# Shift product, state tables and transposes ahead of a scan, in another order on TensorE and VectorE

## The chip, the core and the metric

One core of a Trainium2 chip runs the kernel. The metric is the device time of one execution in microseconds (us), as the median of several runs; a profiled execution of the same program gives the trace. TensorE is PE in the profile (its weight loads are PEld), VectorE is DVE, ScalarE is ACT, GpSimd is POOL, and SyncE is SP, which issues nearly all DMA transfers.

## The reference

One layer of a hybrid decoder, for 1024 positions of width 1024. The part that matters here is the start of the mixer:

```python
mod = (c_act @ w_mod[l] + b_mod[l])[:, None, :]
sh1, sc1, g1, sh2, sc2, g2 = jnp.split(mod, N_MOD, axis=-1)
h = _rms(x, norm1_w[l]) * (1 + sc1) + sh1
proj = h @ w_in[l]
u, q, k, v = jnp.split(proj, [...], axis=-1)
y_ssm = _s5(u, ...)          # 32 groups of 16 channels, 64 complex states each
q, k = rms per head; y_attn = _swa_sink(q, k, v, rel_bias, sinks[l])   # window 128, 8 heads
# in _s5, per group: s[t] = A s[t-1] + B u[t] (complex, diagonal A), y = Re(C s) + D u, then GELU, GLU
x = x + g1 * (concat(rms(y_ssm), rms(y_attn)) @ w_out[l])
# then a gated MLP (width 2816) with a causal convolution of width 3
```

## The kernel before

Everything is float32; a product is made of three products of rounded halves ("hi" and "lo", `mm3`), so each weight or activation tile is split: ACT casts the hi part, DVE subtracts to get the lo part (`split`). Eight PSUM banks are handed out round robin: `mbank` from banks 0 to 3, `abank` from banks 4 to 6.

The stage up to the scan works as follows (lines of the kernel before).

- The loop over the eight 128-row blocks of x (from L239) forms scaled x, the columns sc1 of the modulation, the sums of squares (banks 6, 7), and the first six of eight projections of u. The positions are taken with stride 8: projection j holds positions j, j+8, and so on.
- The normalisation factor `rstd` is made by ACT and DVE in two halves (`rsqrt_mean`, L187). Four DVE transposes (L273) turn it into a column per position, `rc`. Only with `rc` can a projection bank be drained into U (`u_out`, L277). Projections j=6 and j=7 use bank 6 and bank 0 again (L285), so j=7 needs bank 0 drained.
- The columns sh1 of the modulation are eight more DVE reductions over rows of `w_mod`, loaded into three buffers in turn (`emit_mod`, L178, called at L294). They become `shs`, hi and lo (L297, L298). The shift product (`shift_u`, L300) multiplies them with the u weights; DVE reduces it to `Bu`, the bias of u.
- The state tables: A's powers (`PWr`, `PWi`) and B in discrete form (`Bb`, `Bsw`), then four large outer products on DVE (`outer`, called at L437), "table 0" to "table 3", in buffers A5 to A8 (`IB`); each is two products and a sum, with the next buffer as temporary. On PE their transposes W (`emit_wj`, eight of them, drained by ACT into A9 to A12) and the transposes of U (`emit_ut`, eight, drained by ACT with the bias `Bu`, L543) feed the injection products (from L571), whose drain is the scan's input `SC` in buffer S16.
- The C tables (`CAt`, from L589) are five buffers of outer products on DVE, in A5 to A8 and A4, so after the W transposes have read tables 0 to 3. From them PE makes the kernels of the chunk (`ka`), which a transfer takes to DRAM (`kd`, L641).
- The heads: k, v and four pairs of query heads, six of them (`head`), each 2 x 24 products of 512 columns, with weights in U0 to U3, DVE and ACT work on each result (`head_out`), and the queries in `qn` (W1, U4, U5 and others). The scan is 18 calls of `cmac` (from L704), seven DVE instructions each, with temporaries `mt` in buffer A12.

Buffers are named by a tag; a new tile under the tag of an older one waits for the older one's last reader or writer. What is written to the queue of an engine runs in order. That order is chosen ahead of time by a planner that simulates the program with its own costs, in which earlier lines have precedence where nothing else is said. `tc.issue_after(i)` puts instructions of the engine of `i` behind `i` in that engine's queue and binds no other engine. `pe.pin(True)` makes PE keep the written order among the instructions so marked (they show as L99, others as L97). From the shift product to the end of the injection PE is pinned; there `next(h0)` puts one step of a head between: first a head's small row products (`head_w`), then three products per step.

Of the kernel before, what the change touches and what calls it, by code (L numbers as in the profile page):

```python
# [14 lines left out]
ADD, SUB, MUL, MAX, MIN = ALU.add, ALU.subtract, ALU.mult, ALU.max, ALU.min  # L15

L = 1024
D = 1024
# [44 lines left out]
def hymba_kernel(ctx, tc, xT, c, wmod, wu, wkvq, small, consts, relb, pq, wglu, wout, wup, wdn, out):  # L63
# [4 lines left out]
    bank = [pp.tile([128, 512], F32, name=f"bk{i}") for i in range(8)]  # L68
    SIZES = {"HA": 2048, "HB": 2048, "S16": 4096, "XQ": 4096}

    def new(tag, dt=F32):
        return pool.tile([128, SIZES.get(tag, 1024)], dt, tag=tag, name="t" + tag)
# [14 lines left out]
    vec, act, pol, sync = nc.vector, nc.scalar, nc.gpsimd, nc.sync  # L87
# [29 lines left out]
    def tt(eng, o, a, b, op):  # L117
        return eng.tensor_tensor(out=o, in0=a, in1=b, op=op)  # L118
# [7 lines left out]
    def stt(o, a, s, b, op0, op1):  # L126
        return vec.scalar_tensor_tensor(out=o, in0=a, scalar=s, in1=b, op0=op0, op1=op1)  # L127
# [24 lines left out]
    def gh(ap):  # L152
        return ap.rearrange("p (g h) -> p g h", h=16)
# [8 lines left out]
    def S(name, j=0, n=None):  # L162
        o, w = SMALL[name]
        return sm[:, o + j:o + (w if n is None else j + n)]
# [10 lines left out]
    mod = pool.tile([128, 48], F32, name="mod")  # L175
# [11 lines left out]
    def rsqrt_mean(o, t_, ps, n):  # L187

        act.activation(out=o, in_=ps, func=AF.Abs_reciprocal_sqrt, scale=1.0 / n, bias=eps)
        act.activation(out=t_, in_=o, func=AF.Square, scale=math.sqrt(0.5 / n))  # L190
        stt(t_, ps, n * 1e-6, t_, ADD, MUL)
        return stt(o, t_, -1.5, o, ADD, MUL)
# [3 lines left out]
    def abank():  # L196
        ab[0] = (ab[0] + 1) % na[0]
        return bank[4 + ab[0]]
# [9 lines left out]
    def mbank():  # L208
        mb[0] = (mb[0] + 1) % 4
        return bank[mb[0]]  # L210
# [4 lines left out]
    def evac(o, i, key):  # L215
        evc[key] = evc.get(key, -1) + 1
        cpy(pick("E" + key, evc[key]), o, i)
# [21 lines left out]
    for k in range(8):  # L239
# [12 lines left out]
        lasth = stt(lo.r, xk, mods[:, k:k + 1], hi.f, MUL, SUB).ins  # L252
# [12 lines left out]
    rstd = new("X6")  # L265
    rc = new("A4")[:, 0:256].rearrange("p (j x) -> p j x", x=32)
    rtmp = new("A11")
    for h in range(2):
        hs = slice(h * 512, h * 512 + 512)
        normed1 = rsqrt_mean(rstd[:, hs], rtmp[:, hs], bank[6 + h], D).ins  # L270
    for q in range(4):
        qs = slice(32 * q, 32 * q + 32)
        vec.transpose(out=rc[qs], in_=rstd[qs, 256 * q:256 * q + 256].rearrange("p (i j) -> p j i", j=8))  # L273
    U = new("S16")[:, 0:4096]
    Uv = U.rearrange("p (g d h) -> p g d h", d=8, h=16)

# [17 lines left out]
            emit_mod(k, mst[k % 3], cact)  # L294
    shs = pool.tile([128, 16], F32R, name="shs")
    shr = RT(shs.rearrange("p (k s) -> p k s", s=2))
    act.copy(shr.r[:, :, 0], mod[:, 0:8])  # L297
    tt(vec, shr.r[:, :, 1], mod[:, 0:8], shr.f[:, :, 0], SUB)  # L298

    def shift_u():  # L300
        b = mbank()
        for k in range(8):
            s_ = [shs[:, 2 * k + i:2 * k + i + 1].to_broadcast([128, 128]) for i in range(2)]
            pe.matmul(b, s_[0], wus[k][0].r, start=(k == 0), stop=False)
            pe.matmul(b, s_[0], wus[k][1].r, start=False, stop=False)
            pe.matmul(b, s_[1], wus[k][0].r, start=False, stop=(k == 7))
        tmp = new("A9")[:, 0:512]
        tt(vec, gh(tmp), gh(b), S("mod16").rearrange("p (o h) -> p o h", o=1).to_broadcast([128, 32, 16]), MUL)
        vec.tensor_reduce(out=Bu, in_=gh(tmp), axis=mybir.AxisListType.X, op=ADD)

# [105 lines left out]
    def outer(eng, o, tmp, g0, ng, nd, u, v):  # L416
        o = o.rearrange("p (g d h) -> p g d h", d=nd, h=16)
        tmp = tmp.rearrange("p (g d h) -> p g d h", d=nd, h=16)
        shp = [128, ng, nd, 16]

        def bx(w_):
            return gh(w_)[:, g0:g0 + ng, :].rearrange("p g (o h) -> p g o h", o=1).to_broadcast(shp)

        def by(w_):
            return w_[:, g0:g0 + ng, 0:nd].rearrange("p g (d o) -> p g d o", o=1).to_broadcast(shp)

        tt(eng, o, bx(u), by(PWr), MUL)
        tt(eng, tmp, bx(v), by(PWi), MUL)
        return tt(eng, o, o, tmp, ADD).ins

    IB = [new(f"A{5 + i}") for i in range(4)]
    hp = ctx.enter_context(ExitStack())
    hp.enter_context(tc.high_priority(0))
    for i in range(4):
        tmp = new("A10") if i == 3 else IB[i + 1]
        with tc.issue_after(normed1 if i > 1 else lasth):
            built = outer(vec, IB[i], tmp, 8 * i, 8, 8, Bb, Bsw)  # L437
    hp.close()

# [65 lines left out]
    def head(t):  # L505
        w = head_w(t)
        yield
        for h in range(2):
            b = mbank()
            for k in range(8):  # L510
                head_mm(b, w, k, halves[h])
                if k == 7:
                    with pe.pin(False):
                        head_out(t, h, b)
                yield


    pst = ExitStack()
    pst.enter_context(pe.pin(True))
    shift_u()  # L520
    h0 = itertools.chain(*[head(t) for t in range(4)])
    next(h0)

    WJt = [new(f"A{9 + i}") for i in range(4)]

    def emit_wj(i):
        b = abank()
        for q in range(4):
            g = 4 * i + q
            pe.transpose(b[:, q * 128:(q + 1) * 128], IB[g // 8][:, (g % 8) * 128:(g % 8 + 1) * 128], ident)  # L530
        evac(WJt[i // 2][:, (i % 2) * 512:(i % 2 + 1) * 512], b, "W")
    UTt = [None] * 4

    def emit_ut(i):
        if i % 2 == 0:
            UTt[i // 2] = new(f"A{i // 2}")
        b = abank()
        for q in range(4):
            g = 4 * i + q
            pe.transpose(b[:, q * 128:(q + 1) * 128], U[:, g * 128:(g + 1) * 128], ident)  # L540
        for q in range(4):
            g = 4 * i + q
            act.activation(  # L543
                out=UTt[i // 2][:, (g % 8) * 128:(g % 8 + 1) * 128].rearrange("p (r q) -> p q r", r=8), in_=b[:, q * 128:(q + 1) * 128].rearrange("p (q r) -> p q r", r=8),
                func=AF.Identity, bias=Bu[:, g:g + 1],
            )

    for i in range(8):
        emit_ut(i)
        if i == 3:  # L550
            next(h0)
    for i in range(8):
        emit_wj(i)

    def UT(g):
        return UTt[g // 8][:, (g % 8) * 128:(g % 8 + 1) * 128]
# [66 lines left out]
    sync.dma_start(out=vdv[:, :, 128:256], in_=mid.rearrange("p (h v) -> p h v", h=8))  # L623


    ka = new("A12")
    kav = ka.rearrange("p (i d h) -> p i d h", d=8, h=16)
    for i2 in range(2):
        b = abank()
# [10 lines left out]
    for q in range(4):  # L640
        sync.dma_start(out=kd[:, 8 * q:8 * q + 8, 112:240],  # L641
                       in_=ka[32 * q:32 * q + 16, :].rearrange("p (g x) -> p g x", x=128))
# [72 lines left out]
    for h in range(2):  # L715
        for i in range(4):
            q_ = newr(f"H{8 + 4 * h + i}")
            for kv in range(2):
                p0, p1 = slice(kv * 64, kv * 64 + 64), slice(64 - kv * 64, 128 - kv * 64)
                q = q_[:, kv * 512:kv * 512 + 512]  # L720
# [73 lines left out]
    for h in range(2):  # L794
        hs = slice(h * 512, h * 512 + 512)
# [44 lines left out]
    for n in range(8):  # L840
        av = bank[2]
        for kv in range(2):
# [6 lines left out]
            for i2 in range(2):  # L849
# [6 lines left out]
                for i1 in range(2):  # L856
                    i = 2 * i2 + i1
                    vec.tensor_tensor_reduce(  # L858
                        out=P[:, i, :], in0=b[:, i1 * 256:i1 * 256 + w_], in1=Tb[kv][:, i, 256 - w_:256],
# [398 lines left out]
    for s_, (c_, i, p) in enumerate(steps):  # L1258
# [27 lines left out]
        if p == ps_[1] and pend:  # L1286
            put(*pend)
            h, dd = DEST[pend[0]]
# [114 lines left out]
```

## Time and profile before

| | before |
|---|---|
| median of 3 runs | 1131.26 us (1129.86 to 1134.01) |
| profiled execution | 1135.45 us, span 1133.7 us |
| busy, share of the span | PE 92%, DVE 81%, ACT 51%, POOL 24% |
| mean granted TensorE clock | 0.964 |

The profile's times count from the first instruction of the span. The line of a row is that of the instruction in the kernel, which may be a helper: L118 is any two-operand DVE instruction, L127 a scalar-tensor-tensor one, L133 a copy by ACT. In tile names the buffer's number is left out, so tA may be A0 or A12, and tS is S16, the scan's buffer after the injection and U before it.

### The profile page before, as it was taken

The numbers are of one execution on the slowest core, as the hardware profiler recorded it, in microseconds if no ns is written. First come the engines' busy times: TensorE is split into PE (matmuls) and PEld (weight loads), VectorE is DVE, ScalarE is ACT, GpSimd is POOL, SyncE is SP. The second block draws the span as 40 slices with busy tenths as digits, with TensorE's granted clock in tenths as the row PEclk, the third lists the DMA queues.
The fourth block names the chain that finished last, engine by engine and source line by source line (L and its number), as shares of the span: only waits on it lengthen the run. The fifth ranks groups of instructions, "written<-read, shape, count | busy, mean of one in ns | idle before, by whom it ended". The sixth has DMA issues, their size and how long they took to land.

```text
span 1133.7 us, 13323 instructions
## 1 busy us (share of the span) xinstructions
PE 1042.0 (92%) x4676; PEld 820.0 (72%) x4676; DVE 916.1 (81%) x1516; ACT 579.4 (51%) x1013; POOL 274.9 (24%) x166
## 2 busy tenths in 40 slices
PE   6979999477979999959999999999999999989998
PEld 4867777275646677647888888888888778768876
DVE  7984599947879787788778887978796887997985
ACT  5325343457788357735454544554554574434342
POOL 0000000001233202681221222222222033654541
PEclk9989999678999999969999999999999999999999
DMA  9421517004017966322223223242221439622012
GB/s 358 157 93 38 111 56 91 3 29 158 19 38 180 289 185 164 112 93 75 93 75 123 100 95 128 88 154 71 93 84 69 167 141 413 152 39 37 1 38 111
DMA packets 49637, 128.13 MB, mean 113 GB/s; under 512 B 6273, under 2 KB 14241, under 8 KB 49570
## 3 DMA queue, kind: packets, MB, share of 16 engines
q1 hardware_dynamic: 44962, 118.89, 31.4%
q0 software_dynamic: 4608, 8.39, 4.6%
q8 instruction: 36, 0.59, 0.2%
q14 instruction: 31, 0.25, 0.1%
HBM read 105.28 MB, written 21.99 MB: 112 GB/s over the span
## 4 chain that ended last, share of the span: by engine, by line
PE 63%; DVE 26%; DMA 4%; ACT 3%; issue 2%; POOL 1%; SPq 0%; DVEq 0%; ACTq 0%; POOLq 0%
PE bk L97 59%; DVE tA L118 6%; PE bk L99 4%; DVE tH L118 4%; DVE tU L118 3%; DVE tX L127 3%; DMA tW<-in_dram 3%; DVE tS L118 2%; DVE tX L118 1%; DMA tX<-in_dram 1%; DVE tX L180 1%; ACT tU L133 1%; DVE tH L858 1%; ACT tA L543 1%; DVE tXQ L127 1%
## 5 line engine op out<-in xcount | busy, mean ns | idle before, releaser
L97 PE MATMUL bk<-tA,tU 128*128 128x512 f32 x516 | 126.3, 393 | 0.0
L97 PE MATMUL bk<-tU,tU 128*128 128x512 f32 x516 | 121.9, 390 | 1.5 <-DVE tU L118 1.3
L97 PE MATMUL bk<-tH,tU 128*128 128x512 f32 x477 | 117.8, 394 | 0.0
L97 PEld LDWEIGHTS bk<-tU,tU 128*128 128x128 f32 x516 | 96.5, 188 | 23.4 <-DVE tU L118 2.6
L97 PEld LDWEIGHTS bk<-tA,tU 128*128 128x128 f32 x516 | 96.8, 188 | 22.2
L97 PEld LDWEIGHTS bk<-tH,tU 128*128 128x128 f32 x477 | 88.9, 188 | 19.8 <-issue 1.0
L127 DVE SCALAR_TENSOR_TENSOR tX<-tH,sm,tX 128x1023 f32<-128x1023 f32 x66 | 98.2, 1488 | 4.6 <-ACT tX L1129 4.5
L97 PE MATMUL bk<-tA,tXQ 128*128 128x512 f32 x300 | 74.0, 393 | 1.9 <-ACT tH L1082 1.9
L133 ACT CAST tU<-tW 128x512 fp32r<-128x512 f32 (+1 forms) x67 | 47.2, 711 | 53.7 <-DMA tW<-in_dram 21.8
L99 PE MATMUL bk<-tH,tU 128*128 128x512 f32 x267 | 65.5, 400 | 3.5 <-DVE tU L118 2.4
L97 PEld LDWEIGHTS bk<-tA,tXQ 128*128 128x128 f32 x300 | 56.2, 188 | 15.1 <-ACT tH L1082 2.3
L97 PE MATMUL bk<-tXQ,tH 128*128 128x256 f32 (+2 forms) x224 | 52.3, 377 | 15.6 <-DVE att L858 8.9
L118 POOL TENSOR_TENSOR tU<-tW,tU 128x512 fp32r<-128x512 f32 x25 | 36.5, 1469 | 117.2 <-ACT tU L133 110.1
L97 PEld LDWEIGHTS bk<-tXQ,tH 128*128 128x128 f32 x224 | 45.0, 269 | 26.0 <-DVE att L858 13.4
L118 POOL TENSOR_TENSOR tH<-tH,att 128x1024 f32<-128x1024 f32 (+1 forms) x9 | 18.1, 2016 | 188.3 <-DVE att L870 168.8
L99 PEld LDWEIGHTS bk<-tH,tU 128*128 128x128 f32 x267 | 50.1, 191 | 17.1 <-DVE tU L118 3.7
L118 POOL TENSOR_TENSOR tXQ<-tW,tXQ 128x512 fp32r<-128x512 f32 x12 | 49.2, 4107 | 52.2 <-ACT tXQ L133 37.0
L118 DVE TENSOR_TENSOR tX<-tX,tX 128x512 f32<-128x512 f32 (+1 forms) x61 | 58.4, 959 | 1.2 <-DMA tX<-in_dram 0.3
L97 PE MATMUL bk<-tH,tA 128*128 128x512 f32 (+1 forms) x156 | 55.5, 488 | 2.3 <-DVE tH L118 1.1
L118 DVE TENSOR_TENSOR tU<-tW,tU 128x512 fp32r<-128x512 f32 (+2 forms) x43 | 37.9, 882 | 20.9 <-ACT tU L133 20.2
L118 POOL TENSOR_TENSOR tU<-tX,tU 128x512 fp32r<-128x512 f32 x19 | 31.2, 1644 | 81.6 <-ACT tU L133 67.5
L118 DVE TENSOR_TENSOR tU<-tX,tU 128x512 fp32r<-128x512 f32 x37 | 29.6, 807 | 23.9 <-ACT tU L133 23.9
(354 smaller groups left out, 2417.1 us busy)
## 6 DMA issues: line engine op xcount, KB each, us to landing
tW<-in_dram SPq DMA_DIRECT2D x49, 512.0 KB, 3.4
tX<-in_dram SPq DMA_DIRECT2D x47, 512.0 KB, 3.4
tS<-in_dram SPq DMA_DIRECT2D x30, 512.0 KB, 6.3
gd<-tX SPq DMA_DIRECT2D x22, 512.0 KB, 2.9
tA<-in_dram SPq DMA_DIRECT2D x12, 512.0 KB, 10.0
tH<-in_dram SPq DMA_DIRECT2D x12, 512.0 KB, 4.3
tH<-gd SPq DMA_DIRECT2D x8, 512.0 KB, 9.5
tA<-gd SPq DMA_DIRECT2D x8, 512.0 KB, 10.5
```

The lines of the kernel that those rows point to most:

```text
L97: return f(*a, **k)
L99: i = f(*a, **k)
L118: return eng.tensor_tensor(out=o, in0=a, in1=b, op=op)
L127: return vec.scalar_tensor_tensor(out=o, in0=a, scalar=s, in1=b, op0=op0, op1=op1)
L133: act.copy(o, i)
L180: vec.tensor_tensor_reduce(out=st, in0=st, in1=ca, scale=1.0, scalar=S("b_mod", j, 1), op0=MUL, op1=ADD, accum_out=mod[:, j:j + 1],)
L543: act.activation(out=UTt[i // 2][:, (g % 8) * 128:(g % 8 + 1) * 128].rearrange("p (r q) -> p q r", r=8), in_=b[:, q * 128:(q + 1) * 128].r ...
L858: vec.tensor_tensor_reduce(out=P[:, i, :], in0=b[:, i1 * 256:i1 * 256 + w_], in1=Tb[kv][:, i, 256 - w_:256], scale=1.0, scalar=S("sink", 4 ...
```

## The change

Four edits:

1. The point `normed1` moves from the end of the normalisation to the last of the four transposes, so that the eight reductions for sh1 stand behind the transposes in DVE's queue. Table 2 need no longer stand behind `normed1`, only behind the last activation block; table 3's temporary is A12 in place of A10.
2. `shs` is made in two halves of four columns; the shift product's temporary is A3 in place of A9.
3. On PE, W transposes 0 to 5 come first, then the shift product, then U transposes 0 to 3, W transposes 6 and 7, two head steps, U transposes 4 to 7. Before it was: shift product, one head step, U transposes 0 to 3, one head step, U transposes 4 to 7, W transposes 0 to 7.
4. The kernels of the chunk, `ka`, lie in buffer U4 in place of A12. U4 holds B's table before that and a query of head 3 after it.

```diff
     for h in range(2):
         hs = slice(h * 512, h * 512 + 512)
-        normed1 = rsqrt_mean(rstd[:, hs], rtmp[:, hs], bank[6 + h], D).ins
+        rsqrt_mean(rstd[:, hs], rtmp[:, hs], bank[6 + h], D)
     for q in range(4):
         qs = slice(32 * q, 32 * q + 32)
-        vec.transpose(out=rc[qs], in_=rstd[qs, 256 * q:256 * q + 256].rearrange("p (i j) -> p j i", j=8))
+        normed1 = vec.transpose(out=rc[qs], in_=rstd[qs, 256 * q:256 * q + 256].rearrange("p (i j) -> p j i", j=8)).ins
...
-    act.copy(shr.r[:, :, 0], mod[:, 0:8])
-    tt(vec, shr.r[:, :, 1], mod[:, 0:8], shr.f[:, :, 0], SUB)
+    for k in range(0, 8, 4):
+        act.copy(shr.r[:, k:k + 4, 0], mod[:, k:k + 4])
+        tt(vec, shr.r[:, k:k + 4, 1], mod[:, k:k + 4], shr.f[:, k:k + 4, 0], SUB)
...
-        tmp = new("A9")[:, 0:512]
+        tmp = new("A3")[:, 0:512]
...
     for i in range(4):
-        tmp = new("A10") if i == 3 else IB[i + 1]
-        with tc.issue_after(normed1 if i > 1 else lasth):
+        tmp = new("A12") if i == 3 else IB[i + 1]
+        with tc.issue_after(normed1 if i > 2 else lasth):
             built = outer(vec, IB[i], tmp, 8 * i, 8, 8, Bb, Bsw)
...
-    shift_u()
     h0 = itertools.chain(*[head(t) for t in range(4)])
-    next(h0)
...
+    for i in range(6):
+        emit_wj(i)
+    shift_u()
     for i in range(8):
         emit_ut(i)
         if i == 3:
+            emit_wj(6)
+            emit_wj(7)
             next(h0)
-    for i in range(8):
-        emit_wj(i)
+            next(h0)
...
-    ka = new("A12")
+    ka = new("U4")
```

## The prediction

> **What bounds the kernel now.** I read the page's head, then a table of busy times by stretch (columns: length, busy time of PE, PEld, DVE, ACT, POOL, granted clock, share and rate of the DMA engines), cut where the character of the work changes. The fence below it has two rows of the same table for the instructions on the scan's buffer alone (columns in the same order).
>
> ```profile
> span 1133.7 us, 13323 instructions
> core 0: us, PE busy (x) PEld busy (x) DVE busy (x) ACT busy (x) POOL busy (x), PEclk, DMA share, GB/s
> 85.00:106.00 21.00, 19.46 (x107) 15.48 (x107) 6.32 (x23) 10.95 (x35) 0.15 (x1) 0.92 0.15 50
> 106.00:122.00 16.00, 15.81 (x170) 12.84 (x170) 15.26 (x17) 8.75 (x25) 0.32 (x2) 1.00 0.52 80
> 122.00:138.00 16.00, 16.00 (x142) 12.78 (x141) 3.13 (x6) 5.43 (x8) 0.00 (x0) 1.00 0.40 101
> 138.00:198.00 60.00, 58.62 (x297) 45.22 (x295) 59.26 (x141) 25.49 (x38) 0.00 (x0) 1.00 0.45 73
> 198.00:232.00 34.00, 13.40 (x32) 7.54 (x32) 33.37 (x80) 13.17 (x21) 0.00 (x0) 0.59 0.04 4
> ```
>
> ```profile
> 138.00:198.00 60.00, 0.00 (x0) 0.00 (x0) 33.82 (x92) 0.00 (x0) 0.00 (x0) 1.00 0.45 73
> 198.00:232.00 34.00, 0.00 (x0) 0.00 (x0) 13.67 (x36) 0.52 (x1) 0.00 (x0) 0.59 0.04 4
> ```
>
> The reader is to see three things. From 138 to 232 VectorE (DVE) is full: 59.26 + 33.37 = 92.6 of 94 us, of which 47.5 are the scan. Ahead of that, from 85 to 138, DVE works 6.32 + 15.26 + 3.13 = 24.7 of 53 us: it waits 28 us for a chain on TensorE (PE) and ScalarE (ACT). So the full stretch starts late, and what brings its start forward moves its end, if the work in it keeps up. The next view is the timeline, engine by engine (start, length, instructions, in brackets the idle time before and who ended it). First the chain to the scan on PE:
>
> ```profile
> 62.42 0.90 PE L97 MATMUL bk<-tU,tHA 128*128 128x512 f32 x3
> 65.35 3.09 PE L97 MATMUL bk<-tXQ,tH 128*128 128x512 f32 x12
> 73.84 1.67 PE L97 MATMUL bk<-tU,tHA 128*128 128x512 f32 x3 [5.40 <-ACT tS L279]
> 78.71 3.09 PE L97 MATMUL bk<-tXQ,tH 128*128 128x512 f32 x12
> 83.34 0.73 PE L99 MATMUL bk<-tU,shs 128*128 128x512 f32 x2 [1.54 <-ACT shs L297]
> 85.53 3.89 PE L99 MATMUL bk<-tU,shs 128*128 128x512 f32 x10 [1.46 <-DVE shs L118]
> 89.25 2.94 PE L99 MATMUL bk<-tXQ,shs 128*128 128x512 f32 x12
> 96.04 3.14 PE L97 MATMUL bk<-tH,tU 128*128 128x512 f32 x13
> 104.13 0.66 PE L99 MATMUL bk<-cn,tA 128*128 128x128 f32 x4 [0.45 <-ACT tA L543]
> 109.15 2.35 PE L99 MATMUL bk<-tA,tA 128*64 128x128 f32 x32
> 118.70 2.02 PE L99 MATMUL bk<-tA,tA 128*64 128x128 f32 x32
> 193.63 3.42 PE L97 MATMUL bk<-tH,tU 128*128 128x512 f32 x14
> ```
>
> In order: projection j=6 (62.42 to 68.44), j=7 (73.84 to 81.80), the shift product (83.34 to 92.19), U and W transposes (93 to 109.15), four groups of injection products (109.15 to 120.72), then heads until about 197. DVE and ACT beside them:
>
> ```profile
> 60.09 0.69 DVE L127 SCALAR_TENSOR_TENSOR tA<-bk,tA 128x512 f32<-128x512 f32 x1 [4.12 <-ACT tA L190]
> 63.79 0.68 DVE L127 SCALAR_TENSOR_TENSOR tX<-tA,tX 128x512 f32<-128x512 f32 x1
> 66.81 1.28 DVE L180 CUSTOM_DVE_ANT_0 tA<-tA,tX,sm 128x1024 f32<-128x1024 f32 x1
> 68.02 1.22 DVE L118 TENSOR_TENSOR tA<-Bbt,PWr 128x1024 f32<-128x1024 f32 x1
> 69.15 2.35 DVE L118 TENSOR_TENSOR tA<-tU,PWi 128x1024 f32<-128x1024 f32 x2
> 71.74 1.27 DVE L273 STREAM_TRANSPOSE tA<-tX 32x256 f32<-32x256 f32 x2
> 77.94 1.41 DVE L122 TENSOR_SCALAR tS<-bk,tA 128x512 f32<-128x512 f32 x2
> 105.85 1.21 DVE L118 TENSOR_TENSOR tA<-tU,PWr 128x1008 f32<-128x1008 f32 x1 [10.82 <-PE bk L99]
> 124.33 0.69 DVE L118 TENSOR_TENSOR tX<-bk,tX 128x512 f32<-128x512 f32 x1 [2.53 <-PE bk L99]
> 129.09 0.29 DVE L118 TENSOR_TENSOR tA<-tA,ddt 128x128 f32<-128x128 f32 x1 [4.07 <-ACT tA L133]
> 130.88 0.69 DVE L127 SCALAR_TENSOR_TENSOR tX<-bk,tX 128x512 f32<-128x512 f32 x1 [1.50 <-ACT tX L190]
> 138.00 1.43 DVE L118 TENSOR_TENSOR tA<-tS,ep 128x256 f32<-128x256 f32 x4 [4.91 <-DMA kd<-tA]
> 164.89 0.68 DVE L118 TENSOR_TENSOR tU<-bk,tX 128x512 f32<-128x512 f32 x1
> ```
>
> ```profile
> 73.10 3.00 ACT L279 ACTIVATE tS<-bk,tA 128x512 f32<-128x512 f32 x5 [11.80 <-DVE tA L273]
> 83.09 0.20 ACT L297 CAST shs<-mod 128x8 fp32r<-128x8 f32 x1 [0.56 <-DVE mod L180]
> 93.74 2.58 ACT L543 ACTIVATE tA<-bk,Bu 128x128 f32<-128x128 f32 x8 [0.39 <-DVE Bu L309]
> 99.65 6.49 ACT L543 ACTIVATE tA<-bk,Bu 128x128 f32<-128x128 f32 x24 [3.33 <-PE bk L99]
> 105.85 4.13 ACT L133 COPY tA<-bk 128x512 f32<-128x512 f32 x8
> 120.71 1.19 ACT L133 COPY tS<-bk 128x448 f32<-128x448 f32 x4 [2.34 <-PE bk L99]
> ```
>
> The last row's scan input is complete at 121.90; yet the scan's first instruction starts at 138.00, released by the transfer of the kernels of the chunk out of A12, the buffer that the scan's temporaries take next.
>
> **The change, part by part, with its sum.**
>
> *Transposes ahead of the modulation columns, table 2 ahead of both.* Now DVE does the second normalisation step until 64.47, three column reductions (1.21 us apart), table 2 (68.02 to 71.50, 3.48 us), and only then the last two transposes, until 73.01. ACT's drain of bank 0 waits 11.80 us for them and PE 5.40 us for the drain. After the change table 2 may go into DVE's 4.12 us of idle time before 60.09, where its 3.48 fit, and the reductions stand behind the transposes, which end at 64.47 + 1.27 = 65.7. The first drain takes 3.00 / 5 = 0.6, so bank 0 is free at 66.3, before j=6 ends at 68.44: j=7 follows with no gap. It takes 7.96 us now, j=6 took 6.02; without a gap I take 6.02, so j=7 ends at 74.46 in place of 81.80. Gain 7.3, cover 2.1 us (66.3 to 68.44). If the idle time can't take table 2, it goes behind the transposes, and the gain still stands.
>
> *W transposes 0 to 5 ahead of the shift product, which comes in halves.* Eight took 104.13 to 109.15, 5.0 us; six cost 3.8, and PE reaches the shift at 78.2. Is its input there? From 65.7 DVE has two drains (1.41), eight reductions (9.7) and table 3 (3.5): 80.3 at the latest, the first four columns before 76. So the first half product (12 instructions, 2.94) runs until 81.2 and the second finds its columns. The halves add one ACT copy (0.20) and one small subtraction, nothing on this path. The reloads that SyncE (SP) issues for reductions 3 to 7 still follow the reductions that free their three buffers; they move with these, and no other transfer of SP or GpSimd (POOL) is passed. The shift ends at 78.2 + 2 x 2.94 = 84.1 in place of 92.19.
>
> *From the shift to the scan's input.* Bu comes 1.55 us after the shift's end now (92.19 to 93.74), so ACT starts on the U transposes at 85.6. It is the bound there: 32 x 0.27 (6.49 / 24) + two W drains at 0.52 = 9.7, so 95.3. In the trace a group of 24 later head products (one row of it at 96.04) is ahead of some U transposes and ACT idles 3.33 for it; I expect half, since the same PE gap is shorter. Injection starts near 97 in place of 109.15, and with the same 12.75 us to the last drain (109.15 to 121.90) the scan's input is complete at 109.8: gain 12.1. The C tables (DVE, 15.26 us in 106 to 122) no longer wait for all W transposes (the 10.82 us row): the first two can run once the early W transposes have read their buffers, the rest behind W 6 and 7; all are done before 109.
>
> *Kernels of the chunk in U4.* The scan no longer waits for their transfer (4.91). The waits of 2.53, 4.07 and 1.50 before it were also time in which nothing else was ready, because A12 was taken; together 13.0 us in which the scan can now run. The buffer's next user is head 3's query, first written at 164.89, about 27 us behind that transfer; were the cover gone, DVE would stop there for what is missing.
>
> *Sum at the end of the full stretch.* DVE's work behind the scan's input is 3.13 + 92.6 = 95.8; from 109.8 without idle it ends at 205.6, against 232: 26 us. PE sets another limit: its heads end near 197 now, 88 us behind the injection's start; 97 + 88 = 185. Behind them DVE still has what is in 198 to 232 without the scan, 33.37 - 13.67 = 19.7, and some 3 us of latency: 208, so 24 us. I take the later one, 208, and off its 24 us another 2 for the order that the planner will not find: 22. Everything behind 232 starts from this work and PE is the bound of most of it, so I carry all of it to the end. The profiled execution took 1135.45 us, 1.75 around its span of 1133.7; it becomes 1113.5. It lies 4.2 above the median, 1131.26; measured from the median the forecast is 1109. Bounds of what the trace can't show: 7 us (the j=7 gap alone) to 31 (y products start as soon as the scan's 47.5 us are through, ahead of the last heads' outputs).
>
> [...] U and W transposes cycle three PSUM banks, each waiting for an ACT drain of 1.1 us; the granted clock in the like stretch, 106 to 122, was 1.00. [...]
>
> **The rivals.**
> 1. *Scan queued behind head 0.* DVE takes its queue in order. If the planner leaves head 0's output chain ahead of the scan, the waits of 2.53, 4.07 and 1.50 return, 8.1 us: gain 14, 1117. For it: that is the order now. Against: now the scan was not ready before.
> 2. *Everything early.* Gain 31, 1100; for it, the 47.5 us of scan fit well before 185; against, the heads come first in program order.
> 3. *Scan starves the heads.* While the scan fills DVE from 109.8, PE still needs DVE for weight splits and drains of the heads. If the scan stands in the queue as one block of 47.5 us, and two free banks hold 12 us of head products (24 each, at 2.94 / 12), PE stops 35 us: heads end at 220, the stretch at 243, 11 us later than now: 1142. It cancels the gain from a stop of 24 us on, and a stop of 18 to 30 us reads as no change. Against it: in 138 to 198 the two kinds of work stand mixed, 33.82 of 59.26, and PE is busy 58.62 of 60.
> [...]
>
> **How the numbers follow.** A difference under 0.5% (5.7 us) can't be told from none. Forecast (gain 16 to 28): 0.59. Rival 1: 0.14. Rival 2: 0.10. Rival 4: 0.04. Rival 3 as no change: 0.07, as slower: 0.06. Faster is 0.59 + 0.14 + 0.10 + 0.04 = 0.87. The range 1100 to 1123 takes in the forecast, rivals 1 and 4 and half of rival 2: 0.82.
>
> **What would show it.** Right: j=7 starts within 0.5 us of j=6's end and takes about 6 us; the shift product follows W transposes with no wait for its columns and ends near 84; injection starts at 95 to 99; the scan's first instruction starts near 110, released by ACT's drain and not by a transfer; DVE is over 95% busy from there to about 208, and the heads' last product ends near 185. Wrong: reductions or C tables ahead of the shift's columns, so that PE waits there; the scan behind a head output that waits for PE; PE idle for several us between 110 and 185 for a split on DVE; or a later stage that hands the microseconds back.

## The result, and the profile after

The changed kernel takes 1117.19 us (median of 4 runs, 1115.47 to 1119.89), against 1131.69 (median of 4, 1129.86 to 1134.01) for the kernel before beside it: ratio 0.9873, 95% interval 0.9846 to 0.99, a gain of 14.5 us. The profiled execution took 1116.85 us. The table of busy times, cut where the prediction cut it (length, busy PE, PEld, DVE, ACT, POOL, granted clock, DMA share and rate), and below it three stretches of the same kernel for instructions on the scan's buffer alone:

```profile
span 1115.1 us, 13349 instructions
core 0: us, PE busy (x) PEld busy (x) DVE busy (x) ACT busy (x) POOL busy (x), PEclk, DMA share, GB/s
85.00:106.00 21.00, 17.10 (x85) 13.45 (x84) 14.98 (x34) 7.13 (x21) 0.00 (x0) 0.86 0.16 50
106.00:122.00 16.00, 15.06 (x162) 11.88 (x162) 5.91 (x11) 8.19 (x29) 0.48 (x3) 1.00 0.47 76
122.00:138.00 16.00, 16.00 (x142) 12.64 (x141) 15.42 (x37) 7.10 (x13) 0.00 (x0) 1.00 0.40 104
138.00:198.00 60.00, 58.90 (x300) 46.02 (x299) 57.84 (x138) 25.01 (x38) 0.00 (x0) 1.00 0.42 71
198.00:232.00 34.00, 27.82 (x171) 22.52 (x172) 28.24 (x71) 22.99 (x35) 0.00 (x0) 0.80 0.14 25
```

```profile
122.00:138.00 16.00, 0.00 (x0) 0.00 (x0) 11.12 (x28) 0.94 (x4) 0.00 (x0) 1.00 0.40 104
138.00:198.00 60.00, 0.00 (x0) 0.00 (x0) 32.46 (x89) 0.00 (x0) 0.00 (x0) 1.00 0.42 71
198.00:232.00 34.00, 12.70 (x64) 10.33 (x64) 4.89 (x11) 4.18 (x4) 0.00 (x0) 0.80 0.14 25
```

The gain is visible in one row. From 122 to 138 DVE is busy 15.42 us, where it was 3.13 before, and 11.12 of them are scan. PE is as full as before (16.00), so the heads lose nothing by it. From 198 to 232 PE is busy 27.82 us, where it was 13.40: the y products (PE's products with the scan's states, the 64 PE instructions on the scan's buffer) already run there. From 85 to 106, however, PE is busy less than before (17.10, was 19.46). The timeline shows why; PE first (start, length, instructions, in brackets the idle time before and who ended it):

```profile
69.77 1.45 PE L97 MATMUL bk<-tU,tHA 128*128 128x512 f32 x3 [1.72 <-ACT tS L279]
77.33 3.14 PE L99 MATMUL bk<-cn,tA 128*128 128x128 f32 x24
80.23 0.71 PE L99 MATMUL bk<-tU,shs 128*128 128x512 f32 x2
83.74 4.14 PE L99 MATMUL bk<-tU,shs 128*128 128x512 f32 x10 [2.80 <-DVE shs L118]
88.75 0.73 PE L99 MATMUL bk<-tXQ,shs 128*128 128x512 f32 x2 [0.87 <-ACT shs L298]
91.02 4.04 PE L99 MATMUL bk<-tXQ,shs 128*128 128x512 f32 x10 [1.55 <-DVE shs L118]
109.53 0.43 PE L99 MATMUL bk<-tA,tA 128*64 128x128 f32 x2
196.12 0.44 PE L97 MATMUL bk<-tH,tU 128*128 128x512 f32 x1
211.17 0.63 PE L97 MATMUL bk<-tA,tS 128*128 128x128 f32 x2
```

```profile
59.70 0.69 DVE L127 SCALAR_TENSOR_TENSOR tA<-bk,tA 128x512 f32<-128x512 f32 x1 [4.08 <-ACT tA L190]
62.88 1.22 DVE L118 TENSOR_TENSOR tA<-Bbt,PWr 128x1024 f32<-128x1024 f32 x1
67.62 1.31 DVE L273 STREAM_TRANSPOSE tA<-tX 32x256 f32<-32x256 f32 x2
82.41 1.20 DVE L118 TENSOR_TENSOR tA<-tU,PWr 128x1008 f32<-128x1008 f32 x1
83.53 0.15 DVE L118 TENSOR_TENSOR shs<-mod,shs 128x4 fp32r<-128x4 f32 x1
83.60 2.32 DVE L118 TENSOR_TENSOR tA<-tU,PWi 128x1008 f32<-128x1008 f32 x2
89.50 1.22 DVE L118 TENSOR_TENSOR tU<-tW,tU 128x1024 fp32r<-128x1024 f32 x1
90.81 0.15 DVE L118 TENSOR_TENSOR shs<-mod,shs 128x4 fp32r<-128x4 f32 x1
122.31 1.43 DVE L118 TENSOR_TENSOR tA<-tS,ep 128x256 f32<-128x256 f32 x4 [10.30 <-ACT tS L133]
```

```profile
98.06 3.32 ACT L542 ACTIVATE tA<-bk,Bu 128x128 f32<-128x128 f32 x12 [2.84 <-DVE ep L118]
121.74 1.19 ACT L133 COPY tS<-bk 128x448 f32<-128x448 f32 x4 [2.35 <-PE bk L99]
219.36 1.28 ACT L759 ACT_TABLE_LOAD   x1
234.28 1.28 ACT L868 ACT_TABLE_LOAD   x1
503.30 1.28 ACT L1213 ACT_TABLE_LOAD   x1 [1.01 <-DVE tX L127]
```

The shift product does follow the W transposes at 80.23, but stands three times for its columns, and ends at 95.06 (91.02 + 4.04), 2.9 us later than before. On DVE, C tables (the 128x1008 rows) and a weight split stand between the reductions and the subtractions that complete `shs`. The injection starts at 109.53 (before 109.15). The scan nevertheless starts at 122.31, 15.7 us earlier, released by ACT's drain of its own input: nothing stands between the input and the scan any more. The three table loads on ACT mark the first gelu (before at 236.00), the first exponential of the attention (before at 253.60), and the first Silu of the MLP (before at 523.81). The last row of the PE rows above is the first of the y products, at 211.17; in the kernel before it was this one:

```profile
234.59 0.63 PE L97 MATMUL bk<-tA,tS 128*128 128x128 f32 x2
```

### The profile page after: what moved, and what is told of

It reads as the page before. It is cut to its first block, busy times and chain, and to the rows that moved or that the text cites. A ratio compares the mean times of both kernels' runs of the same rounds, so it can differ in the third digit from the quotient of the medians.

```text
span 1115.1 us, 13349 instructions
## 1 busy us (share of the span) xinstructions
PE 1037.8 (93%) x4676; PEld 818.9 (73%) x4676; DVE 914.0 (82%) x1517; ACT 579.5 (52%) x1014; POOL 271.5 (24%) x166
## 4 chain that ended last, share of the span: by engine, by line
PE 45%; DVE 11%; issue 1%; DMA 1%; ACT 1%; POOL 0%; DVEq 0%; ACTq 0%; POOLq 0%; SPq 0%
PE bk L97 45%; DVE tA L118 2%; DVE tH L118 2%; DVE tU L118 2%; DVE tX L127 1%; DVE tX L118 1%; DMA tX<-in_dram 1%; DVE tS L118 1%; DVE tXQ L127 0%; DMA tW<-in_dram 0%; DVE tW L127 0%; PE bk L99 0%; DVE tHA L118 0%; ACT tH L133 0%; DVE tXQ L118 0%
## 5 line engine op out<-in xcount | busy, mean ns | idle before, releaser
L97 PE MATMUL bk<-tXQ,tH 128*128 128x256 f32 (+2 forms) x224 | 48.7, 359 | 6.3 <-DVE att L861 5.2
```

What stands on the lines that cost most here:

```text
L97: return f(*a, **k)
```

## The experiments

**Which edit makes the gain.** Four kernels beside the kernel before (1131.09 on their chip). First the kernel before with edit 4 alone:

```diff
-    ka = new("A12")
+    ka = new("U4")
```

> The kernel before, with the kernels of the chunk in U4 as the only edit. Theory A (the gain of the change comes from the scan's early start alone; the new order in front of the scan gives nothing): the scan's input is complete near 122 as before, the scan starts at once instead of at 138.0, released by a drain on ACT and not by a transfer, and nearly the whole gain is here: 1112 to 1118 us. Rival B (the transfer's 4.9 us are all that this edit frees; the rest came from the tables and the shift product being out of the way): about 1127 us.

Measured: 1121.52 us, ratio 0.9916 (0.9893 to 0.9939). One line gives 9.6 us of the 14.5. Its scan starts at the same time as the changed kernel's, with none of the other edits:

```profile
122.00 0.76 DVE L118 TENSOR_TENSOR tA<-tS,ep 128x256 f32<-128x256 f32 x2
```

The time lies between the two that I had expected (theory A 1112 to 1118, rival B about 1127). Up to the attention, though, this one line gives the whole gain: its y products start even earlier than the changed kernel's 211.17, and its first exponential comes 0.4 us behind the changed kernel's 234.28:

```profile
208.93 0.80 PE L97 MATMUL bk<-tA,tS 128*128 128x128 f32 x2 [0.28 <-DVE tS L740]
```

```profile
234.65 1.28 ACT L865 ACT_TABLE_LOAD   x1
```

What the other three edits add to it, some 5 us by the two ratios, whose intervals overlap, is not there yet at that mark. In the profiles the two kernels part behind it (first Silu at 507.60 and 503.30), by about as much as two profiles of the same program do (last experiment). The reverse, the changed kernel with `ka` back in A12:

> The changed kernel with the kernels of the chunk back in A12, so edits 1 to 3 alone. Theory A: the scan again waits for the transfer, near 139, and the time is that of the kernel before within 3 us: 1130 to 1134. Rival B: most of the gain stays, 1121 to 1124 us.

Measured: 1136.95 us, ratio 1.0047 (1.0029 to 1.0066): 5.9 us slower than before. The three front edits alone give nothing, since the scan waits for the same transfer as before:

```profile
138.46 0.76 DVE L118 TENSOR_TENSOR tA<-tS,ep 128x256 f32<-128x256 f32 x2 [4.74 <-DMA kd<-tA]
```

The time is above the 1130 to 1134 that I expected. Why these edits alone cost time is open: up to the first exponential (252.85, before 253.60) the trace shows no loss. The gains of the edits do not add up: U4 is worth 9.6 us alone, and by the ratios 1.0047 and 0.9873 some 20 us on top of the other three.

Next the kernel before with edit 4 and `normed1` at the last transpose, tables 2 and 3 both behind it, PE's old order and the undivided `shs`:

```diff
-        normed1 = rsqrt_mean(rstd[:, hs], rtmp[:, hs], bank[6 + h], D).ins
+        rsqrt_mean(rstd[:, hs], rtmp[:, hs], bank[6 + h], D)
...
-        vec.transpose(out=rc[qs], ...)
+        normed1 = vec.transpose(out=rc[qs], ...).ins
...
-    ka = new("A12")
+    ka = new("U4")
```

> The kernel before with U4 and with the reductions behind the transposes (the first half of edit 1; tables 2 and 3 behind the transposes too), but with the old order on PE and the shift's columns in one piece. If the transposes were the step that held PE, j=7 starts by 68.5 and lasts 6 us, the shift product ends near 88 and injection starts near 105, 4 us ahead of the kernel before: 3 to 4 us less than with U4 alone. If DVE's work ahead of the shift's columns is the bound and not the transposes, j=7 is early but the shift product still ends at 91 to 92, and the time is that of U4 alone within 1 us.

Measured: 1122.43 us, ratio 0.9919 (0.99 to 0.9939), no better than edit 4 alone. The transposes end at 65.80, as I had predicted for the changed kernel, j=7 follows without a gap, and PE then stands for the columns:

```profile
83.24 1.22 PE L99 MATMUL bk<-tU,shs 128*128 128x512 f32 x2 [9.19 <-ACT shs L297]
```

What is gained ahead of the shift product is waited away in front of it: the columns on DVE bind, not the projections. So in the changed kernel the C tables were put behind them:

```diff
-        tt(vec, shr.r[:, k:k + 4, 1], ...)
+        cols = tt(vec, shr.r[:, k:k + 4, 1], ...).ins
...
     later.enter_context(tc.issue_after(built))
+    later.enter_context(tc.issue_after(cols))
```

> The changed kernel with one more edge: the C tables stand behind the shift's columns in DVE's queue. If C tables in front of the columns are what cost the shift product its gain (5.8 us of them stand ahead of the second half's columns), the columns come near 85 in place of 90.8, the shift product ends near 89 in place of 95.1, injection starts near 104 in place of 109.5, and the time falls 4 to 6 us below that of the change, to 1111 to 1113. Rival: the C tables only move in between the shift product and the U transposes and delay Bu; then injection stays at 108 to 110 and the time within 1 us of the change, 1117.

Measured: 1116.62 us, ratio 0.9871 (0.9846 to 0.9896).

```profile
85.70 0.15 DVE L118 TENSOR_TENSOR shs<-mod,shs 128x4 fp32r<-128x4 f32 x1
117.85 1.43 DVE L118 TENSOR_TENSOR tA<-tS,ep 128x256 f32<-128x256 f32 x4 [10.29 <-ACT tS L133]
```

The columns come 5.1 us earlier and the scan starts 4.5 us earlier. The first exponential comes only 1.6 earlier (232.71), the time is the same. So the front did what I expected (injection at 105.07), and the expected time of 1111 to 1113 was wrong.

**Which part of the front, and where its gain goes.** Three kernels beside 1131.97 for the kernel before. The changed kernel with edit 1 taken out except for table 3's temporary:

```diff
-        normed1 = vec.transpose(out=rc[qs], ...).ins
+        vec.transpose(out=rc[qs], ...)
...
-        with tc.issue_after(normed1 if i > 2 else lasth):
+        with tc.issue_after(normed1 if i > 1 else lasth):
```

(and `normed1` again at the end of `rsqrt_mean`).

> U4, the shift's columns in halves, the temporaries A3 and A12 and the new order on PE, but normed1 and table 2 as in the kernel before (reductions ahead of the last transposes). Its planned order on PE behind the y products is the same, instruction by instruction, as that of the run with the C tables behind the columns. Theory C (from U4 alone to the whole change, the 5 us come from the order that the planner happens to give the later stages): the last transposes end near 73 again, j=7 starts near 74, injection is not earlier than 109, and still the time is 1115 to 1119 us. Rival D (they come from the front: reductions behind the transposes, tables early): 1120 to 1124.

Measured: 1118.47 us, ratio 0.989 (0.9864 to 0.9916), within the changed kernel's interval: without edit 1 the time can't be told from the changed kernel's. (Injection starts at 108.17, a little earlier than I expected.) The other way, the C tables behind the columns as above, and table 2 behind the transposes:

```diff
-        with tc.issue_after(normed1 if i > 2 else lasth):
+        with tc.issue_after(normed1 if i > 1 else lasth):
```

> The change with the C tables behind the shift's columns and table 2 behind the transposes. Its front is as early as that of the run with the C tables behind the columns (scan's first instruction near 118), its planned order on PE behind the y products the same as that of the run with U4 and the transposes (1122.4 us). Theory C: 1120 to 1124 in spite of the early front. Rival D: 1114 to 1118.

Measured: 1113.93 us (1112.59 to 1115.78), ratio 0.9847 (0.9822 to 0.9872). This is the fastest complete version; it beats the kernel before by 18.0 us, and its median the changed kernel's by 3.3, with overlapping intervals. Theory C, that the order behind the y products sets the end, gave 1120 to 1124 and falls: in the traces PE runs the same sequence here as in the run with U4 and the transposes from 213 us on, and this kernel is fast all the same. Rival D does not come out whole either: it gave 1120 to 1124 for the run before this one, which took 1118.47, with an interval that reaches into that range. Last, everything behind the columns: tables 2 and 3 too, W transposes 0 to 3 ahead of the shift product and 4 to 7 after U transpose 3:

```diff
-        with tc.issue_after(normed1 if i > 2 else lasth):
+        with tc.issue_after(cols if i > 1 else lasth):
...
-    for i in range(6):
+    for i in range(4):
         emit_wj(i)
...
-            emit_wj(6)
-            emit_wj(7)
+            for j_ in range(4, 8):
+                emit_wj(j_)
```

> The change with nothing but drains and reductions ahead of the shift's columns on DVE: tables 2 and 3 and the C tables stand behind the columns, and on PE W transposes 0 to 3 come ahead of the shift product, 4 to 7 behind U transpose 3. This is what the prediction's sum assumed: columns near 80, shift product done near 85, injection near 99, the scan's first instruction near 112. If the sum was right but for the columns, the first exponential comes 7 to 10 us ahead of the change's 234.3 and the time is 1107 to 1111 us. If the heads on PE and what DVE does behind them are a bound of their own and the order of the later stages weighs as much, the first exponential gains 2 to 5 us and the time lies between 1112 and 1120.

Measured: 1116.87 us, ratio 0.9876 (0.9849 to 0.9904). On DVE and ACT:

```profile
81.79 0.16 DVE L118 TENSOR_TENSOR shs<-mod,shs 128x4 fp32r<-128x4 f32 x1
115.84 1.43 DVE L118 TENSOR_TENSOR tA<-tS,ep 128x256 f32<-128x256 f32 x4 [7.72 <-ACT tS L133]
```

```profile
227.81 1.28 ACT L869 ACT_TABLE_LOAD   x1
503.43 1.28 ACT L1214 ACT_TABLE_LOAD   x1
```

The columns, the scan and the first exponential are 9.0, 6.5 and 6.5 us earlier than in the changed kernel. The first Silu is at 503.43, where the changed kernel has 503.30. Between the two marks, all that the front gained is given back. The first exponential gained nearly the 7 to 10 us that I expected if the sum was right but for the columns; the time is in the range for the other case (1112 to 1120). The two kernels do not run quite the same order in that stage: from 251 us on the planner placed some PE instructions differently.

**What takes it back.** In that stage the changed kernel has a stretch from 330 to 370 us in which the DMA engines are full (share 0.88, 0.97, 1.04 and 1.04 in steps of 10 us), among others with 16 modulation loads of 512 KB (`emit_mod`, called at L942). Two kernels with these loads cut to a quarter (the reductions keep their length and don't use them, so the output is not the layer's), one from the changed kernel, one from the kernel with early columns, beside 1131.51 for the kernel before:

```diff
-        sync.dma_start(out=st, in_=wmod[j])
+        light = 24 <= j < 40
+        w_ = 256 if light else 1024
+        sync.dma_start(out=st[:, 0:w_], in_=wmod[j][:, 0:w_])
...
-            out=st, in0=st, in1=ca, ...
+            out=st, in0=ca if light else st, in1=ca, ...
```

> The changed kernel with the 16 modulation loads of the output projection (512 KB each) cut to a quarter; their reductions keep their length and no longer use the loaded values, so the output differs. In the changed kernel's trace the DMA engines are full from 330 to 370 us (share 0.86 to 1.08, 14.7 MB from 325 to 385), and 6.3 MB go away here, some 21 us of transfer at 300 GB/s. Theory E (these full DMA engines hold what the front gains): faster than the changed kernel by 3 us or more, 1108 to 1114. Theory F (the queues' order behind the first exponential decides): within 3 us of it, 1114 to 1120.

> The kernel with early columns, cheap loads as in the run before: the same 16 loads cut to a quarter. With full loads its first exponential came 6.5 us earlier than in the changed kernel and the first Silu at the same time. Theory E: with the DMA engines free the 6.5 us come through, so it ends 4 to 7 us before the run with light loads alone. Theory F: the gain is lost again although the loads are light; it ends within 2 us of that run.

Measured: 1111.53 us, ratio 0.9816 (0.9796 to 0.9836), and 1110.09 us, ratio 0.9809 (0.9791 to 0.9826). The stretch from 350 to 400 in the changed kernel and in the first of them:

```profile
350.00:400.00 50.00, 44.91 (x174) 32.91 (x173) 37.29 (x62) 22.37 (x34) 5.15 (x6) 0.93 0.77 233
```

```profile
350.00:400.00 50.00, 46.73 (x188) 34.20 (x187) 37.15 (x60) 23.14 (x35) 5.14 (x6) 0.97 0.62 164
```

With less traffic PE does 14 products more there, and the ratio falls by 0.0057, some 6 us, with intervals apart: cutting the loads gains time, as theory E said. (The planner also ordered some instructions between 335 and 377 us differently, so not all of the 6 us need be the traffic.) On the lead of the early columns theory E wanted 4 to 7 us between the two light kernels and theory F up to 2; the medians lie 1.4 apart, with overlapping intervals. Their profiles lie further apart. First exponential and first Silu, light loads alone first, then with early columns:

```profile
234.54 1.28 ACT L870 ACT_TABLE_LOAD   x1
499.68 1.28 ACT L1215 ACT_TABLE_LOAD   x1
```

```profile
228.82 1.28 ACT L871 ACT_TABLE_LOAD   x1
496.70 1.28 ACT L1216 ACT_TABLE_LOAD   x1 [1.02 <-DVE tX L127]
```

With light loads 3.0 of 5.7 us of lead are left at the first Silu; with full loads nothing was left of 6.5. That difference is about as large as the one between two profiles of the same program (next experiment). So it is not settled whether the full DMA engines are part of what swallows the front's gain; nothing here shows that they are all of it. Which wait swallows it is open. With full loads the lead of the early columns is 8.0 us at the last reciprocal of the attention (344 us) and gone by 382, where the norm of the attention's second half begins (`branch_norm`, L822); with light loads it is 6.0 us at the first of these marks and 4.4 at the second.

**How much one profile says.** The kernel before once more:

> The kernel before, for a second profile. The first one's time, 1135.45, lay above the timed runs (1125.96 to 1135.16). If the first profile is typical, the projection j=7 again starts after 5.40 us of waiting and the scan near 138.0, and the last milestones move with the granted clock alone; a time of 1126 to 1132 then shows that some 4 of the 18.6 us between the two profiles are the clock.

Measured: 1133.05 us, outside the 1126 to 1132 that I had set as the sign for the clock. The mean granted clock was lower than in the first profile (0.959 against 0.964) although the time was 2.4 us shorter, so the clock alone does not explain the first profile's length. ACT's marks of the first profile of the kernel before, and of this one:

```profile
253.60 1.28 ACT L865 ACT_TABLE_LOAD   x1
523.81 1.28 ACT L1210 ACT_TABLE_LOAD   x1 [1.01 <-DVE tX L127]
```

```profile
253.51 1.28 ACT L865 ACT_TABLE_LOAD   x1
519.82 1.28 ACT L1210 ACT_TABLE_LOAD   x1 [1.02 <-DVE tX L127]
```

The early stages repeat within 1.1 us (j=7 after 5.44 us of waiting, scan at 138.63). From the first exponential to the first Silu the same program took 270.2 us once and 266.3 the other time. Differences of up to 4 us in that stage, read from one profile each, are therefore not evidence; the front's lost 6.5 us are more than that, and the medians agree with them.

## Why the prediction was right, and where not

The direction and the range (1100 to 1123) held; the forecast of 1109 was 8 us too low, and the gain of 14.5 us is below the 16 to 28 of the forecast's own band. Of the two mechanisms in the sum, one held (with U4 the scan no longer waits for the transfer), and the other, a front 12 us earlier, did not come about at all. That the time still fell inside the range is partly luck: a mechanism that I had named as a rival made up most of what was missing, and the 1117 that I gave to rival 1 came out without it. By its own steps:

- **Transposes and table 2: the planner chose otherwise.** DVE's idle time ahead of 59.70 stayed empty (4.08); the sum of table 1 (60.31), a product of table 2 (62.88) and the sum of table 2 (66.11) went between the normalisation steps, and the transposes ended at 68.93 (67.62 + 1.31), not 65.7. I had two places for table 2, and it took a third. After the 1.72 us of waiting j=7 lasted until 77.5, also because of a slower clock (0.58 and 0.56 from 70 to 74, last section), so the gain was 4.3 and not 7.3. Where it was kept behind the transposes with U4 as the only other edit, they ended at 65.8 and j=7 had no gap, as worked out, and it bought nothing (1122.43 against 1121.52). I had also misread the trace of before: a table is two products and a sum, so the three rows from 68.02 to 71.50 are two products of table 2 and one of table 3, and table 2's sum is a later row, at 75.46. Their length, which the sum used, is the same.
- **Columns by 80.3: this is the step that failed.** They came at 83.7 and 91.0. I had counted the drains, the reductions and table 3 ahead of them, and put the C tables far behind; an `issue_after` that binds them to table 3 alone let the planner fill DVE with them. That was on my list of what would prove me wrong. The 9.7 us for eight reductions were also short: with tables 2 and 3 and the C tables out of the way they still waited for the reloads of their three buffers, four times and 2.3 us in all, and the columns came at 81.95.
- **From Bu to the scan's input: right in length, not in place.** From ACT's first drain with `Bu` to the injection I had 11.4 us (85.6 to 97), the trace has 11.5 (98.06 to 109.53); from there to the last drain I had 12.75, the trace has 13.4. The injection came 12.5 us later than predicted. Terms one to three together gave -1.0 us in place of 12.1 (scan input at 122.93, before 121.90).
- **The buffer U4: right.** The scan starts 0.6 us after the start of the drains that complete its input; no transfer and no head chain stands before it, so rival 1 did not occur. U4's next user never stopped DVE: from 125 to 215 us its only waits are four of 0.63 us or less, all for PE.
- **The end of the full stretch: two errors of opposite sign.** PE's limit was the heads' end plus 22.7 us. The 3 us of latency in it were an estimate that no run shows; PE's first wait behind its heads was 2.38 us in the trace of before and is 1.10 here. The heads end at 196.6 (196.12 + 0.44), as before and not at 185, since the injection did not move; that makes 219.3, a gain of 12.7. But the y products no longer wait behind the last heads' outputs: they start at 211.17, among them, where they started at 234.59. That is rival 2's mechanism, and it brings the gain to 19.3 at the first exponential (234.28 against 253.60), 6.6 us more. So of the 9.3 us that were missing from the 22 of my sum, 6.6 were made up by the rival to which I gave 0.10. The run with U4 alone shows that the buffer brings this about: there the y products start at 208.93 and the first exponential is at 234.65, without any of the front edits.
- **Rival 3, the starved heads:** PE 58.90 of 60 from 138 to 198; it did not happen.
- **Rival 4, a slower clock, to which I gave 0.04:** no run shows one from 106 to 122, where the last transposes and the injection products run; the granted clock is 1.00 there again, as in the trace of before. The 0.86 from 85 to 106 lies beside the waits of 2.80, 0.87 and 1.55 us for the columns; that they cause it is not shown.
- **Carried to the end: right in the profiles, less in the medians.** 19.3 us at the first exponential are 18.6 between the profiled executions, but 14.5 between the medians. The first profile of before was a long one, 1135.45 against a median of 1131.69, and 4 us of its length lie in a stage that varies by as much. I took the gain from that profile and the base from the median. Of the 7.8 us that the gain fell short of 22.3, 2.7 are the stretch up to the first exponential, 0.7 the rest of the profile, 4.1 this, and 0.3 rounding.

## What to carry to other kernels

A buffer whose next user waits for a slow reader can cost more than the order of the work in front of it: here its name alone was worth 9.6 us, and three edits of the order alone were worth nothing. Look first for the DVE or PE instruction whose idle time a transfer out of a reused buffer ends, and give the tenant another buffer. When a step is moved earlier, ask what the planner will put in the place that becomes free, and bind the ready but unimportant work behind the urgent one in so many words; here that brought the columns 5.1 us forward, though not the end. A gain far ahead of the end has to be looked for again at each later mark, and a difference between two profiles that is no larger than the spread of that stage between two profiles of the same program shows nothing.

## What the runs showed of the hardware

Nearly equal idle times were followed by different clocks. The changed kernel's PE stood 1.72 us ahead of j=7, and ran the next 4 us at a granted clock of 0.58 and 0.56; the kernel with light loads has the same instructions up to there, stood 1.69 us, and ran at 1.00 (first the changed kernel's rows, then the other's):

```profile
70.00:72.00 2.00, 2.00 (x6) 1.71 (x7) 2.00 (x5) 2.00 (x4) 0.00 (x0) 0.58 0.31 68
72.00:74.00 2.00, 2.00 (x7) 1.64 (x6) 2.00 (x4) 0.03 (x1) 0.00 (x0) 0.56 0.69 248
```

```profile
70.00:72.00 2.00, 2.00 (x8) 2.00 (x9) 2.00 (x5) 2.00 (x4) 0.00 (x0) 1.00 0.30 74
72.00:74.00 2.00, 2.00 (x10) 2.00 (x9) 2.00 (x4) 0.20 (x1) 0.00 (x0) 1.00 0.85 283
```

The run with the C tables behind the columns stood 1.69 us ahead of j=7 as well, and its clock was 1.00 from 68 to 74. Behind a longer wait, the 5.40 us of the kernel before, j=7 ran at 0.50 from 74 to 78. What made the clock of the changed kernel fall behind its 1.72 us is not shown.

Runs of one program also differ in their mean granted clock, and the longer ones mostly have the lower clock: of the kernel before, on one chip, the run with 0.971 took 1125.96 us and the three with 0.959 took 1133.27 to 1135.16; with edit 4 alone, 0.974 went with 1118.81 and 0.966 with 1126.54. That the clock is the cause of the difference is not shown.
